# Moving the triangular substitution to GpSimd, a state update by multiply-add, and scan copies planned first

## The chip, the cores and the metric

The kernel runs on one core of one Trainium2 chip. The metric is the device time of one execution in microseconds (us), lower is better. Five engines work side by side, each through its own queue in a fixed order: TensorE (PE, matmuls; PEld is its weight load), VectorE (DVE), ScalarE (ACT), GpSimd (POOL) and SyncE (SP, which here issues the DMAs).

## The reference, cut to what matters

One layer of a hybrid encoder trunk over 1024 tokens of width 1024. A modulated RMSNorm feeds one wide projection; three token mixers read it: an mLSTM, a gated long convolution by FFT, and a bidirectional RWKV-7 scan. Their outputs are gated, projected, merged and added to the input. The change lies in the RWKV-7 branch. Each of its 16 heads carries a 64x64 state, once forwards and once backwards:

```
def step(state, inp):
    r_t, w_t, k_t, v_t, kk_t, a_t = inp
    sa = jnp.einsum('bhij,bhj->bhi', state, -kk_t)
    state = (state * w_t[:, :, None, :] + sa[..., None] * (kk_t * a_t)[:, :, None, :]
             + v_t[..., None] * k_t[:, :, None, :])
    return state, jnp.einsum('bhij,bhj->bhi', state, r_t)
...
y_fwd = rwkv7_scan(r_h, dec_h[:, :, 0], k_dir[:, :, 0], v_h, kk, a_h[:, :, 0], reverse=False)
y_bwd = rwkv7_scan(r_h, dec_h[:, :, 1], k_dir[:, :, 1], v_h, kk, a_h[:, :, 1], reverse=True)
```

## The kernel before, in words

The 1024 tokens are cut into 16 chunks of 64. Within a chunk the recurrence becomes a few 64x64 matmuls if the inverse of a unit triangular matrix is at hand; across chunks the state is handed on. Heads go in 8 pairs (two heads fill 128 partitions, both directions lie side by side), and each pair's chunks are treated in two groups g of 8.

For a pair, `load` and `prep` (L1445, L1534) build the decayed keys and queries `ar`, `bk` for one group and direction. `tphase` (L1597) makes the inverses of one group: matmuls `pq`, a DVE transposition into `Ab` (L1625), a DMA of a start matrix into `Tb` (L1628), then the substitution loop of 31 steps (L1630 to L1638). Step l multiplies a column of `Ab` by a finished row of `Tb` into the scratch tile `tm` and adds `tm` onto the rows below. So there are 62 instructions, each waiting for the one before it, with n*m elements per partition (n = 31-l, m = l//2+1): 2856 for all products and as many for all sums. Two more transpositions (L1641, L1644), the matmuls `pw` and `px`, and ACT copies (the last at L1663) then fill `tt`, which the scan multiplies with.

`scan` (L1740) walks the 16 chunks of a pair. A chunk is a chain: matmuls U; DVE copy `us` (L1769); matmuls SA; copies into `SV` by DVE (L1775) and ACT (L1776); matmuls SN; the new state S1 = (SN + S0) * pc as two DVE instructions (`sn`, L1787 and L1788, by the helper at L476); copies of S1 into `SV` by DVE (L1800) and ACT (L1801), with which the next chunk's U begins. `setup` (L1666) prepares the matrices G and B for two chunks at a time. `outputs` adds up the chunk's result `y`.

Four things set the order. `weave` (L72) traces the scan and, between its steps (four to a chunk), pieces of the other generators: the loop of the own pair's second group is traced from step 8 on, that of the next pair's first group from step 41 on, and matmuls of the big projection (`gemm`, L343, with weights split by ACT at L333 and POOL at L334) are filled in evenly. From the traced program a planner writes each engine's queue: among the instructions that are ready by its own cost estimates it takes the one with the lowest number, which is the place in the traced program; `high_priority(n)` lowers the number by n, `tphase` runs 400 ahead (`TP`), and `in_turn` (L391) keeps a group of matmuls together with 10**6. On the chip each queue then runs strictly in that order. Third, tiles have a fixed number of buffers: `ar` and `bk` have 8, so the next pair's group can only be prepared when the current pair's chunks of that group are done, and the PSUM tile of `banks` (L401) has one buffer, which `pq`, `pw`/`px` and the `pgr` and `ptv` of `setup` take in turn. Fourth, SP's queue issues the DMAs, among them the one into `Tb`.

POOL has little in its queue in the scan: `wl` (L334), the memset of `s` in `prep` (L1555), and in some pairs a few casts.

Of the kernel before, what the change touches and what calls it, by code (L numbers as in the profile page):

```python
# [11 lines left out]
F32 = mybir.dt.float32  # L12
# [13 lines left out]
SA, SB = 100, 16  # L26
# [86 lines left out]
class Row0:  # L113
# [133 lines left out]
    def first(self, w1t, bf):  # L247

        acc = self.ts(w1t[:, 0:1], 0.0, MUL)
        for i in range(1, 17):  # L250
            acc = self.tt(acc, w1t[:, i:i + 1], ADD)
        return self.act(acc, bf, 0)
# [33 lines left out]
class Trunk:  # L286
# [104 lines left out]
    def in_turn(self, calls, ins=None):  # L391

        for f in calls:
            if ins is None:
                ins = f()  # L395
                continue
            with self.tc.issue_after(ins.ins), self.tc.high_priority(10 ** 6):
                ins = f()  # L398
        return ins

    def banks(self, name):  # L401

# [1194 lines left out]
    def tphase(self, cx, g):  # L1597

        nc, rp = self.nc, self.rp
        x2 = lambda n: self.ep.tile([128, 16, 32], F32, name=n, tag="x2", bufs=3)
        q, q21 = x2("quad"), self.ep.tile([128, 16, 32], F32, name="q21", tag="q21", bufs=1)
        pq = [x.rearrange("p (c t) -> p c t", t=CL) for x in self.banks("pq")]

        def blocks():

            for d in range(2):
                for c in range(8):
                    bt, al = cx["bk"][g, d, c], cx["ar"][g, d, c]  # L1610
                    for h in range(2):
                        hs = slice(64 * h, 64 * h + 64)
                        yield partial(nc.tensor.matmul, pq[d][64 * h:64 * h + 32, c, :], bt[hs, 0, 0:32], al[hs, 0, :],
                                      start=True, stop=True)
                        yield partial(nc.tensor.matmul, pq[d][64 * h + 32:64 * h + 64, c, 0:32], bt[hs, 0, 32:64],
                                      al[hs, 0, 32:64], start=True, stop=True)
        self.in_turn(blocks())
        for d, ps in enumerate(pq):
            u = slice(d * 8, d * 8 + 8)
            nc.scalar.copy(q[:, u, :], ps[:, :, 0:32])  # L1620
            for h in range(2):
                nc.scalar.copy(q21[64 * h:64 * h + 32, u, :], ps[64 * h:64 * h + 32, :, 32:64])
        yield
        Ab = self.ep.tile([128, 32, 32], F32, name="Ab", tag="Ab", bufs=1)
        nc.vector.transpose(Ab.rearrange("p t (g u) -> p t g u", g=2),  # L1625
                            q.rearrange("p u t -> p t u").unsqueeze(2).broadcast_to([128, 32, 2, 16]))
        Tb = x2("Tb").rearrange("p a b -> p (a b)").rearrange("p (t s) -> p t s", s=16)
        nc.sync.dma_start(Tb, self.A["tinit"])  # L1628
        tm = rp.tile([128, 136], F32, name="tm", tag="tm", bufs=1)
        for l in range(31):  # L1630
            n, m = 31 - l, l // 2 + 1
            x = tm[:, 0:n * m].rearrange("p (a b) -> p a b", b=m)
            self.tt(x, Ab[:, l + 1:32, l].unsqueeze(2).broadcast_to([128, n, m]),
                    Tb[:, l, 0:m].unsqueeze(1).broadcast_to([128, n, m]))
            o = Tb[:, l + 1:32, 0:m]
            self.tt(o, o, x, ADD)
            if l % 5 == 4:
                yield  # L1638
        tt = self.tt_t[g]
        t1 = x2("t1").rearrange("p a b -> p (a b)").rearrange("p (v s) -> p v s", s=16)  # L1640
        nc.vector.transpose(t1.rearrange("p v s -> p s v"), Tb.rearrange("p t s -> p s t"))  # L1641
        t1 = t1.rearrange("p (g u) s -> p u s g", g=2)
        t2 = x2("t2")
        nc.vector.transpose(t2.rearrange("p u (s g) -> p u s g", g=2), t1)  # L1644
        yield

        W = x2("W")
        pw, px = (x.rearrange("p (u t) -> p u t", t=32) for x in self.banks("pwx"))
        r = [slice(64 * h, 64 * h + 32) for h in range(2)]
        self.in_turn(partial(nc.tensor.matmul, pw[64 * h + 32:64 * h + 64, u, :], q21[r[h], u, :], t1[r[h], u, :],  # L1650
                             start=True, stop=True) for u in range(16) for h in range(2))
        for h in range(2):
            r1, r2 = slice(64 * h, 64 * h + 32), slice(64 * h + 32, 64 * h + 64)
            nc.scalar.copy(W[r2], pw[r2])
            nc.scalar.copy(tt[r1, :, 0:32], t2[r1])
            nc.scalar.copy(tt[r2, :, 32:64], t2[r2])
        yield
        r = [slice(64 * h + 32, 64 * h + 64) for h in range(2)]
        self.in_turn(partial(nc.tensor.matmul, px[64 * h:64 * h + 32, u, :], W[r[h], u, :], t2[r[h], u, :],
                             start=True, stop=True) for u in range(16) for h in (1, 0))  # L1660
        for h in range(2):
            r1 = slice(64 * h, 64 * h + 32)
            nc.scalar.copy(tt[r1, :, 32:64], px[r1])  # L1663
        yield
# [75 lines left out]
    def scan(self, cx, nx):  # L1740

        nc, rp = self.nc, self.rp
        S0 = None
        y = rp.tile([128, T], F32, name="y", tag="y", bufs=1)
        hsl = (slice(0, 64), slice(64, 128))

        def chunk(m):

            G, B, SV, at = cx["set"]
            at = at[m % 2]  # L1750
            step = at[1] - at[0]
            return G, B, SV, at, slice(at[0], at[1] + (1 if step > 0 else -1) if at[1] + step >= 0 else None, step)
        now, late = chunk(0), None
        for m in range(16):
            g, c, j = m // 8, m % 8, m % 2
            tt = self.tt_t[g]
            ar = [cx["ar"][g, d, c] for d in range(2)]
            G, B, SV, at, both = now
            if j == 0:
                ahead = self.setup(cx, m // 2 + 1) if m < 14 else self.setup(nx, 0) if nx else iter(())  # L1760
            ch = self.ps.tile([128, 4, 2, CL], F32, name="pch", tag="c", bufs=2)
            U, SA, SN, py = (ch[:, i] for i in range(4))

            ins = self.in_turn(partial(nc.tensor.matmul, U[hsl[h], d], G[:, j, d, h, 0:64], SV[:, h, at[d]],
                                       start=True, stop=True) for d in range(2) for h in (1, 0))
            if late:
                late[0](ins)
            us = self.sm.tile([128, 2, CL], F32, name="us", tag="us", bufs=2)
            nc.vector.tensor_copy(us, U)  # L1769
            ins = self.in_turn(partial(nc.tensor.matmul, SA[hsl[h], d], tt[hsl[h], 8 * d + c, :], us[hsl[h], d],  # L1770
                                       start=True, stop=True) for d in range(2) for h in range(2))
            if late:
                late[1](ins)
            late = None
            nc.vector.tensor_copy(SV[0:64, 0, both], SA[0:64])  # L1775
            nc.scalar.copy(SV[0:64, 1, both], SA[64:128])  # L1776
            yield
            next(ahead, None)
            yield
            self.in_turn(partial(nc.tensor.matmul, SN[hsl[h], d], B[:, j, d, hsl[h]], SV[:, h, at[d]],  # L1780
                                 start=True, stop=True) for d in range(2) for h in (1, 0))
            S1 = self.sm.tile([128, 2, 64], F32, name="sn", tag="sn", bufs=3)
            pc = cx["pc"][g][:, :, c:c + 1].broadcast_to([128, 2, 64])
            if m == 0:
                self.tt(S1, SN, pc)
            else:
                self.tt(S1, SN, S0, ADD)  # L1787
                self.tt(S1, S1, pc)  # L1788
            late = self.outputs(y, py, m, S0, ar, now)
            S0 = S1  # L1790
            if m < 15:
                now = chunk(m + 1)

            if m in (7, 15):
                late[1](late[0](None))
                late = None
            if m < 15:

                SV, at = now[2], now[4]
                nc.vector.tensor_copy(SV[0:64, 0, at], S1[0:64])  # L1800
                nc.scalar.copy(SV[0:64, 1, at], S1[64:128])  # L1801
            yield
            next(ahead, None)
            yield
        cx["y"] = y
        if nx:
            cx["y"] = self.dram.tile([128, T], F32, name="yd", tag="yd", bufs=2)
            nc.sync.dma_start(cx["y"], y)
# [107 lines left out]
```

## Time and profile before

| what | value |
|---|---|
| three runs, median (lowest to highest) | 2187.35 us (2179.21 to 2191.44) |
| the profiled execution | 2200.05 us |
| its span | 2198.3 us |
| TensorE clock granted, mean | 0.956 |
| scan of the 8 pairs | about 929 to 1990 us of the span |

The profile is one execution. Its times count from the start of the span; 1.75 us of the execution lie outside it. A group of instructions is shown as line, engine, operation, out<-in, shape and count, then busy time and the mean of one in ns, then the idle time of its engine before them and what ended that. A row of one tile has the shortest, the median and the longest duration in ns, and the first and the last start. A row of the timeline has the start and the duration in us, and in brackets the engine's idle time before it.

### The profile page before, as it was taken

The page shows a single profiled execution, that of the slowest core. Times are in us where ns is not written, and L with a number is a line of the kernel's source. Part 1 is how long each engine was busy: PE and PEld are TensorE (multiplying, and loading weights), DVE is VectorE, ACT ScalarE, POOL GpSimd, SP SyncE. Part 2 cuts the span into 40 slices and gives each one's busy share as a digit, 9 for nine tenths or more (in the row PEclk, how much of TensorE's full clock was granted, in tenths as well). Part 3 has the DMA queues.
Part 4 walks back from the last instruction along what each step waited for, and adds up shares of the span by engine and source line. Part 5 has one row for each costly group of instructions (what it writes and reads, how often), then busy time and mean ns, then how long its engine had stood idle before and what let it go on. Part 6 is the DMA issues. An engine that isn't in the chain of part 4 may idle for free. (4 is left out here: it accounts for less than half of the span.)

```text
span 2198.3 us, 45984 instructions
## 1 busy us (share of the span) xinstructions
PE 1994.0 (91%) x17098; PEld 1509.2 (69%) x17098; DVE 1634.6 (74%) x4754; ACT 1103.2 (50%) x2558; POOL 424.3 (19%) x485
## 2 busy tenths in 40 slices
PE   6999899999989899899989999999898887897998
PEld 4666777787868677666766676666666665675786
DVE  4854999988447947788787888868887888764536
ACT  5557356454242115664665756667466564532221
POOL 2211311122222432311101111111114411010200
PEclk9999999999999999999998999999899998897999
DMA  8211222334465345321322333224143542445623
GB/s 255 70 67 59 78 77 90 112 101 127 143 200 172 119 138 163 124 68 61 130 79 93 117 106 102 92 81 136 52 155 118 187 144 63 159 143 175 196 89 129
DMA packets 169384, 262.19 MB, mean 119 GB/s; under 512 B 17863, under 2 KB 87335, under 8 KB 169160
## 3 DMA queue, kind: packets, MB, share of 16 engines
q1 hardware_dynamic: 169160, 259.25, 36.3%
q8 instruction: 135, 2.21, 0.4%
q14 instruction: 89, 0.73, 0.1%
HBM read 181.06 MB, written 78.12 MB: 118 GB/s over the span
## 5 line engine op out<-in xcount | busy, mean ns | idle before, releaser
L334 POOL TENSOR_TENSOR wl<-wraw,wh 128x256 fp32r<-128x256 f32 x408 | 371.5, 915 | 1488.6 <-ACT wh L333 1464.8
L351 PE MATMUL pg<-hh,wh 128*128 128x512 f32 x1440 | 601.5, 418 | 20.9 <-ACT wh L333 11.8
L352 PE MATMUL pg<-hh,wl 128*128 128x512 f32 x1440 | 594.3, 413 | 16.4 <-POOL wl L334 16.3
L353 PE MATMUL pg<-hl,wh 128*128 128x512 f32 x1440 | 592.4, 412 | 1.9 <-DVE hl L565 1.8
L351 PEld LDWEIGHTS pg<-hh,wh 128*128 128x128 f32 x1440 | 278.7, 194 | 88.9 <-ACT wh L333 15.1
L352 PEld LDWEIGHTS pg<-hh,wl 128*128 128x128 f32 x1440 | 279.3, 194 | 78.0 <-POOL wl L334 22.2
L353 PEld LDWEIGHTS pg<-hl,wh 128*128 128x128 f32 x1440 | 278.1, 193 | 62.0 <-DVE hl L565 2.8
L333 ACT CAST wh<-wraw 128x256 fp32r<-128x256 f32 x408 | 162.7, 404 | 220.6 <-PE pg L353 122.1
L476 DVE TENSOR_TENSOR tm<-Ab,Tb 128x126 f32<-128x126 f32 (+22 forms) x496 | 145.4, 293 | 4.4 <-DMA Tb<-in_tinit 2.7
L476 DVE TENSOR_TENSOR Tb<-Tb,tm 128x126 f32<-128x126 f32 (+22 forms) x496 | 144.2, 291 | 1.9
L473 DVE SCALAR_TENSOR_TENSOR st<-pg,hmu,st 128x511 f32<-128x511 f32 (+1 forms) x130 | 80.9, 636 | 27.9 <-ACT e L424 17.6
L476 DVE TENSOR_TENSOR G<-pgr,gmask 128x512 f32<-128x512 f32 x128 | 85.4, 679 | 17.0 <-PE pgr L398 17.0
L457 ACT ACTIVATE st<-pg 128x512 f32<-128x512 f32 x74 | 44.2, 597 | 99.9 <-PE pg L353 95.0
L1684 ACT COPY G<-ar 64x128 f32<-64x128 f32 x256 | 64.3, 295 | 48.4 <-DVE G L476 46.6
L473 DVE SCALAR_TENSOR_TENSOR st<-st,pg 128x512 f32<-128x512 f32 x80 | 54.3, 679 | 35.7 <-PE pg L353 12.7
L398 PE MATMUL pgr<-ar,bk 64*128 64x128 f32 x896 | 76.9, 287 | 0.0
L141 DVE SCALAR_TENSOR_TENSOR row<-row 64x1 f32<-64x1 f32 x393 | 72.7, 208 | 2.1
L1769 DVE COPY us<-pch 128x128 f32<-128x128 f32 x128 | 36.3, 283 | 45.8 <-PE pch L398 45.5
L395 PEld LDWEIGHTS pch<-SV,G 128*64 128x64 f32 x256 | 25.3, 139 | 65.5 <-ACT SV L1801 52.3
L395 PE MATMUL pch<-SV,G 128*64 128x64 f32 x256 | 43.2, 252 | 27.7 <-ACT SV L1801 26.2
L476 DVE TENSOR_TENSOR dw<-dw,dw 128x512 f32<-128x512 f32 x92 | 67.1, 760 | 0.9
L395 PEld LDWEIGHTS pch<-SV,B 128*64 128x64 f32 x256 | 25.3, 139 | 60.1 <-ACT SV L1776 50.1
(677 smaller groups left out, 4228.4 us busy)
## 6 DMA issues: line engine op xcount, KB each, us to landing
wraw<-in_w_in SPq DMA_DIRECT2D x340, 128.0 KB, 2.3
low<-lora SPq DMA_DIRECT2D x32, 512.0 KB, 4.1
sig<-st SPq DMA_DIRECT2D x48, 256.0 KB, 2.6
st<-sig SPq DMA_DIRECT2D x48, 256.0 KB, 3.5
wraw<-in_w_br SPq DMA_DIRECT2D x68, 128.0 KB, 2.8
adw<-in_ada_w SPq DMA_DIRECT2D x16, 512.0 KB, 7.1
x<-in_x SPq DMA_DIRECT2D x8, 512.0 KB, 6.1
hx<-st SPq DMA_DIRECT2D x16, 256.0 KB, 2.0
```

What stands on the lines that cost most here:

```text
L141: self.ops.append(lambda: self.nc.vector.scalar_tensor_tensor(o, a, s, b, op0=op0, op1=op1))
L333: self.nc.scalar.copy(hi, raw)
L334: self.nc.gpsimd.tensor_tensor(lo, raw, hi.bitcast(F32), op=SUB)
L351: nc.tensor.matmul(p, wh, hh, start=(k == 0), stop=False)
L352: nc.tensor.matmul(p, wl, hh, start=False, stop=False)
L353: nc.tensor.matmul(p, wh, hl, start=False, stop=(k == n - 1))
L395: ins = f()
L398: ins = f()
L457: self.nc.scalar.activation(o, p, AF.Tanh, scale=0.5)
L473: return self.nc.vector.scalar_tensor_tensor(out, in0, s, in1, op0=op0, op1=op1)
L476: return self.nc.vector.tensor_tensor(out, a, b, op=op)
L1684: nc.scalar.copy(G[0:64, :, d, h, 0:64], cx["al"][g, d, b % 4][hsl[h]])
```

## The change

Three edits, all in the RWKV-7 branch. The two instructions of each step of the substitution loop are issued on GpSimd and not on VectorE, with the same operands. The new state is formed as S1 = SN * pc + S0d, by one scalar_tensor_tensor for each direction, where S0d = S0 * pc (with this chunk's pc) has been made on GpSimd from the state before, right after that state was ready; the first chunk still has SN * pc alone. And the scan's copies (`us`, both pairs of `SV` copies) and the instructions that make S1 are traced with a priority of 10**6; the multiplication on GpSimd is not.

```
+    def first(self):
+
+        return self.tc.high_priority(10 ** 6)
...
         for l in range(31):
             n, m = 31 - l, l // 2 + 1
             x = tm[:, 0:n * m].rearrange("p (a b) -> p a b", b=m)
-            self.tt(x, Ab[:, l + 1:32, l].unsqueeze(2).broadcast_to([128, n, m]),
-                    Tb[:, l, 0:m].unsqueeze(1).broadcast_to([128, n, m]))
+            nc.gpsimd.tensor_tensor(x, Ab[:, l + 1:32, l].unsqueeze(2).broadcast_to([128, n, m]),
+                                    Tb[:, l, 0:m].unsqueeze(1).broadcast_to([128, n, m]), op=MUL)
             o = Tb[:, l + 1:32, 0:m]
-            self.tt(o, o, x, ADD)
+            nc.gpsimd.tensor_tensor(o, o, x, op=ADD)
...
-            nc.vector.tensor_copy(us, U)
+            with self.first():
+                nc.vector.tensor_copy(us, U)
...
-            nc.vector.tensor_copy(SV[0:64, 0, both], SA[0:64])
-            nc.scalar.copy(SV[0:64, 1, both], SA[64:128])
+            with self.first():
+                nc.vector.tensor_copy(SV[0:64, 0, both], SA[0:64])
+                nc.scalar.copy(SV[0:64, 1, both], SA[64:128])
...
-            pc = cx["pc"][g][:, :, c:c + 1].broadcast_to([128, 2, 64])
-            if m == 0:
-                self.tt(S1, SN, pc)
-            else:
-                self.tt(S1, SN, S0, ADD)
-                self.tt(S1, S1, pc)
+            pc = cx["pc"][g][:, :, c:c + 1]
+            with self.first():
+                if m == 0:
+                    self.tt(S1, SN, pc.broadcast_to([128, 2, 64]))
+                else:
+                    for d in range(2):
+                        self.stt(S1[:, d], SN[:, d], pc[:, d], S0d[:, d])
+            if m < 15:
+
+                S0d = rp.tile([128, 2, 64], F32, name="sd", tag="sd", bufs=2)
+                pc = cx["pc"][(m + 1) // 8][:, :, (m + 1) % 8:(m + 1) % 8 + 1]
+                nc.gpsimd.tensor_tensor(S0d, S1, pc.broadcast_to([128, 2, 64]), op=MUL)
...
-                nc.vector.tensor_copy(SV[0:64, 0, at], S1[0:64])
-                nc.scalar.copy(SV[0:64, 1, at], S1[64:128])
+                with self.first():
+                    nc.vector.tensor_copy(SV[0:64, 0, at], S1[0:64])
+                    nc.scalar.copy(SV[0:64, 1, at], S1[64:128])
```

## Prediction, made blind

> **What bounds the kernel now.** I read the page's first part, then the view by windows, then the timeline of two halves of a pair, and last the rows of the tiles that the change touches. The page:
>
> ```profile
> PE 1994.0 (91%) x17098; PEld 1509.2 (69%) x17098; DVE 1634.6 (74%) x4754; ACT 1103.2 (50%) x2558; POOL 424.3 (19%) x485
> ```
>
> Over the span POOL is the idle engine. Only the scan changes, so the next rows are windows (start and end, length, then busy time and count of PE, PEld, DVE, ACT and POOL, then the granted clock): the stretch just ahead of the scan, the scan, and inside the scan one substitution loop and the 17 us after it.
>
> ```profile
> 866.00:929.00 63.00, 57.07 (x371) 43.61 (x369) 51.47 (x126) 38.58 (x74) 17.81 (x16) 1.00 0.35 119
> 929.00:1990.00 1061.00, 958.49 (x12168) 705.19 (x12167) 845.54 (x2465) 625.80 (x1555) 169.66 (x215) 0.95 0.33 108
> 1262.00:1306.00 44.00, 41.99 (x526) 29.98 (x526) 40.55 (x139) 24.23 (x62) 6.13 (x9) 1.00 0.23 74
> 1306.00:1323.00 17.00, 16.79 (x249) 12.39 (x249) 8.12 (x20) 11.54 (x24) 0.73 (x1) 1.00 0.44 155
> ```
>
> In the scan DVE is busy 80% of the time and PE 90%. But DVE is full only while a loop runs (40.55 of 44 us); behind it DVE is half idle (8.12 of 17) and PE does projection matmuls while the scan stands still. So something other than the load of DVE paces the scan. The timeline of DVE, then of ACT, over two halves of a pair shows it: `us` marks the first chunk of a half, `Ab` and the first and last `tm` and `Tb` the loop, the `tt` copies its end.
>
> ```profile
> 1261.51 0.27 DVE L1769 COPY us<-pch 128x128 f32<-128x128 f32 x1
> ...
> 1269.03 2.00 DVE L1625 STREAM_TRANSPOSE Ab<-quad 128x1024 f32<-128x1024 f32 x1
> ...
> 1271.18 0.19 DVE L476 TENSOR_TENSOR tm<-Ab,Tb 128x31 f32<-128x31 f32 x1
> 1271.30 0.27 DVE L1775 COPY SV<-pch 64x128 f32<-64x128 f32 x1
> 1271.50 0.19 DVE L476 TENSOR_TENSOR Tb<-Tb,tm 128x31 f32<-128x31 f32 x1
> 1271.61 1.22 DVE L1564 TENSOR_TENSOR_SCAN s<-smask,s 128x520 f32<-128x520 f32 x1
> ...
> 1305.69 0.16 DVE L476 TENSOR_TENSOR Tb<-Tb,tm 128x16 f32<-128x16 f32 x1
> ...
> 1322.68 0.69 DVE L1498 TENSOR_SCALAR a<-phs 128x512 f32<-128x512 f32 x1 [1.06 <-PE phs L1433]
> 1323.29 0.28 DVE L1769 COPY us<-pch 128x128 f32<-128x128 f32 x1
> ...
> 1335.43 1.99 DVE L1625 STREAM_TRANSPOSE Ab<-quad 128x1024 f32<-128x1024 f32 x1
> ...
> 1337.45 0.21 DVE L476 TENSOR_TENSOR tm<-Ab,Tb 128x31 f32<-128x31 f32 x1
> 1337.69 0.21 DVE L476 TENSOR_TENSOR Tb<-Tb,tm 128x31 f32<-128x31 f32 x1
> ...
> 1378.28 0.16 DVE L476 TENSOR_TENSOR Tb<-Tb,tm 128x16 f32<-128x16 f32 x1
> ...
> 1394.50 0.29 DVE L1769 COPY us<-pch 128x128 f32<-128x128 f32 x1 [1.08 <-PE pch L398]
> ```
>
> ```profile
> 1314.45 1.17 ACT L1663 COPY tt<-pwx 32x512 f32<-32x512 f32 x2
> ...
> 1386.78 1.15 ACT L1663 COPY tt<-pwx 32x512 f32<-32x512 f32 x2
> ```
>
> ```profile
> L1625 DVE STREAM_TRANSPOSE Ab<-quad x16: 1952/1986/2106, 866.9 to 1895.7; 128x1024 f32<-128x1024 f32 x16
> ```
>
> Each half is one ring of five stretches. From its first `us` to `Ab`: 7.5 and 12.1 us, mean 9.8. `Ab` to the first `tm`: 2.1. The loop: 34.7 and 41.0, mean 37.8. From there to the end of the `tt` copies: 9.8 and 9.5, mean 9.6. From there to the next half's `us`: 7.7 and 6.6, mean 7.1. Sum 66.5 us; the 16 `Ab` lie (1895.7 - 866.9) / 15 = 68.6 us apart, so these two halves stand for all. The ring closes through buffers: the next group's `bk` waits for the chunks of the group before, and G and `pgr` of the next chunks wait for the PSUM tile that `pw` and `px` hold. The loop is over half of it. On DVE it is slow because other DVE work stands between its links (1271.18, 1271.30, 1271.50, 1271.61), not because its instructions are.
>
> **Part one: the loop on POOL.**
>
> ```profile
> 929.00:1990.00 1061.00, 271.06 (x930) 0.95 0.33 108
> ```
>
> This is the window view for the tile `tm`: 930 instructions, 15 loops of 62, take 271 us of DVE. All leave DVE's queue. What they cost on POOL no row shows; the nearest are POOL's own (tile rows with shortest, median and longest ns; a group; a memset; one line of the timeline):
>
> ```profile
> L334 POOL TENSOR_TENSOR wl<-wraw,wh x408: 715/742/10347, 34.0 to 2091.0; 128x256 fp32r<-128x256 f32 x136
> L930 POOL TENSOR_TENSOR dml<-kt,dmh x4: 1272/1286/1297, 636.4 to 640.6; 128x512 fp32r<-128x512 f32 x4
> L334 POOL TENSOR_TENSOR wl<-wraw,wh 128x256 fp32r<-128x256 f32 x165 | 140.4, 854 | 773.2 <-ACT wh L333 753.2 <-PE ptv L1693 11.3 <-issue 4.5
> L1555 POOL MEMSET s<- x32: 106/113/120, 747.0 to 1829.9; 128x8 f32 x32
> 1664.52 1.18 POOL L334 TENSOR_TENSOR wl<-wraw,wh 128x256 fp32r<-128x256 f32 x1 [0.22 <-POOL wl L334]
> ```
>
> 256 more elements cost 1286 - 742 = 544 ns, 2.125 ns each, which leaves 198 ns for the instruction. A loop is 62 x 0.198 + 5712 x 0.002125 = 12.3 + 12.1 = 24.4 us (from below, with the memset's 113 ns as the constant, 19.1). To this comes the hand-over from each to the next: 0.03 us on DVE (1337.45 + 0.21 to 1337.69), at most the 0.22 of the one POOL row. I take 0.08, nearer to DVE, since the POOL row may hold a second wait: 5.0 us. In the scan `wl` takes 854 ns on average against 742, 112 ns for waiting on DVE; DVE loses most of its two-input work, so I take half, 0.056 x 62 = 3.5. Strangers in POOL's queue: 165 `wl` in 1061 us are 5.9 in 38 us, 4.4 us; the new S0d has 128 elements, 0.47 us, about 4.6 of them, 2.2. These fill ten of the hand-overs, -0.8. Loop: 38.7 us, 0.9 more than now. Far ends: 19.1 + 1.9 + 0 + 4.4 = 25 and 24.4 + 13.6 + 6.9 + 6.6 = 51.
>
> Queues: the loop is put behind and ahead of `wl`, the memsets of `s` and `SV`, and S0d. While its first instruction waits for `Ab` or for the DMA into `Tb`, `wl` waits behind it, and so PE's matmuls with `wl`; the idle time in the row (773 of 1061 us) is the cover. No DMA moves; SP's queue keeps its order.
>
> The Trainium skill, "SBUF — State Buffer", section "Who interferes with whom", says that a DVE instruction with two SBUF inputs and a GpSimd one that reads SBUF exclude each other for a whole instruction. The trace agrees (`wl` has 10347 ns at the longest), and by the rule the loop comes out as in the second slower rival below.
>
> **Part two: the new state.** Rows of the tiles `sn`, `SV`, `y`, and one scalar_tensor_tensor from PSUM:
>
> ```profile
> L476 DVE TENSOR_TENSOR sn<-pch,sn x120: 236/287/294, 941.3 to 1985.8; 128x128 f32<-128x128 f32 x120
> L476 DVE TENSOR_TENSOR sn<-sn,pc x120: 236/284/858, 943.4 to 1986.2; 128x128 f32<-128x128 f32 x120
> L1800 DVE COPY SV<-sn x120: 171/209/1305, 935.5 to 1982.2; 64x128 f32<-64x128 f32 x120
> L476 DVE TENSOR_TENSOR y<-y,pch x128: 165/210/226, 1002.6 to 1987.7; 128x64 f32<-128x64 f32 x128
> L473 DVE SCALAR_TENSOR_TENSOR E<-pnm,cols,cmask x64: 322/334/352, 276.1 to 408.9; 128x128 f32<-128x128 f32 x64
> ```
>
> Two dependent instructions, 0.57 us, become two independent ones of 64 columns, between 0.21 (`y`) and 0.33 (`E`) each; I take 0.24, 0.48 in all: -0.1 us a chunk. S0d is ready long before, unless POOL lags: it has the time of U, SA and SN. If it is late, DVE's queue stops at the first multiply-add with `prep` behind it, and the copies of S1 wait.
>
> **Part three: copies first.** Only the planned order changes. A scan instruction on DVE can now be passed by none that is ready: the `us` at 1323.29 stood behind an `a<-phs` of 0.69 us. I take 0.3 us saved for each of five scan instructions of a chunk, with 0 and 0.69 as ends. Inside the ring's loop the scan isn't on the path; outside, about two chunks of each half are: 2 x (5 x 0.3 + 0.1) = 3.2 us. `prep` and G, passed by now, are the price; DVE, lighter by 271 us, pays it.
>
> **Sum.** A half changes by 0.9 - 3.2 = -2.3 us, 15 halves by -35. The first loop lies ahead of the scan (DVE 51.47 of 63 us busy) and the last eight chunks have no loop behind them: I count both at nothing, since what the one may lose (0.9) the other gains (8 x 0.1). Of the profiled execution's 2200.05 us (span 2198.3, and 1.75 around it) 2165 are left; the median of the runs is 0.9942 of it, so 2152.
>
> **The rivals.** Slower by the hand-over (0.15): POOL's wait for itself is 0.22 us. That adds 62 x 0.14 = 8.7 to each loop, a half is 6.4 longer, 15 x 6.4 = +96: 2296, 2283 as a median. It decides from 0.08 + 2.3 / 62 = 0.12 us on. For it speaks the one row; against it that DVE needs 0.03.
>
> Slower by the shared port (0.13): if each POOL instruction of the loop meets half of a two-input DVE instruction, like this one,
>
> ```profile
> L476 DVE TENSOR_TENSOR bk<-tmp,s x64: 394/412/952, 854.8 to 1864.9; 128x256 f32<-128x256 f32 x64
> ```
>
> it costs 0.21 x 62 = 13.0 in place of 3.5; a half is 7.2 longer, +108: 2308, as a median 2295. It decides where half of them are hit. For it: `SV<-sn`, 209 ns, once took 1305. Against it: most `wl` take their 742.
>
> No change (0.17): the copies were seldom late or the path runs through ACT and `setup` at the restart, so the 3.2 us aren't there, and the loop is as long as now. Then 2187, and it is also the case that the priority does nothing.
>
> Much faster (0.15): the constant is the memset's, hand-over 0.03: 19.1 + 1.9 + 3.5 + 4.4 + 2.2 - 0.3 = 30.8, 7.0 less; a half -10.2, in all -153. PE's 958 of 1061 us busy, though by modelled ends, leave 103: about -100, 2100, as a median 2088.
>
> **How the numbers follow.** My forecast has 0.40, with its own range of 2120 to 2176. Measurement tells 0.5% (11 us) from no change. Faster: 0.40 + 0.15 = 0.55; same 0.17; slower 0.28. The range leaves out a tenth on each side, the fastest of the last rival with the lowest loop and the slow ones above their prices: 2080 to 2285.
>
> **What would show it.** The tiles `tm` and `Tb` on POOL, mean near 0.39 us; loop near 39 us from first `tm` to last `Tb`; `Ab` 66 us apart and not 68.6; DVE's busy time in the scan near 845 - 271 - 0.1 x 120 = 560; no wait of the scan for S0d over half a microsecond. Wrong: `Ab` over 69 us apart, or gaps over 0.12 us between POOL's links, or scan instructions on DVE stretched beside POOL, as `SV<-sn` was.

## The result, and the profile after

The changed kernel takes 2418.28 us (median of 4 runs, 2415.08 to 2425.05) where the kernel before, on the same chip, takes 2187.38. The ratio is 1.1065 with a 95% interval of 1.1025 to 1.1105: slower by 231 us, where 2152 was forecast. The profiled execution has a span of 2413.3 us against 2198.3. First the page, then three windows: the scan, one loop, and the part of that loop in which VectorE stands (columns as in the prediction).

```profile
PE 2014.5 (83%) x17098; PEld 1517.7 (63%) x17098; DVE 1441.0 (60%) x3762; ACT 1100.2 (46%) x2556; POOL 846.5 (35%) x1597
```

```profile
960.00:2200.00 1240.00, 960.10 (x11755) 698.20 (x11753) 643.20 (x1495) 608.89 (x1503) 546.22 (x1193) 0.88 0.28 90
1330.00:1364.00 34.00, 16.03 (x147) 11.85 (x145) 11.25 (x28) 8.55 (x21) 28.51 (x69) 0.73 0.13 40
1348.00:1363.60 15.60, 2.30 (x21) 1.89 (x17) 0.39 (x2) 0.03 (x1) 13.43 (x37) 0.50 0.06 20
```

The same work (PE 2014.5 us busy, 1994.0 before) is spread over a longer time. Before, DVE was busy for 40.55 of the 44 us of a loop and PE for 41.99. Now for half of a loop nothing runs but POOL: DVE has 0.39 us of work in 15.60, PE 2.30, and PE's granted clock there is 0.50. The rows of the loop itself show nothing slow (groups, then one tile's row):

```profile
L1640 POOL TENSOR_TENSOR Tb<-Tb,tm 128x126 f32<-128x126 f32 (+22 forms) x496 | 204.0, 411 | 35.6
L1637 POOL TENSOR_TENSOR tm<-Ab,Tb 128x126 f32<-128x126 f32 (+22 forms) x496 | 196.0, 395 | 49.9 <-DVE Ab L1629 8.9
```

```profile
L1629 DVE STREAM_TRANSPOSE Ab<-quad x16: 1899/2026/2101, 854.2 to 2083.7; 128x1024 f32<-128x1024 f32 x16
```

The links take 395 and 411 ns, as predicted (0.39 us). But `Ab` comes every (2083.7 - 854.2) / 15 = 82.0 us, not 68.6. What lies in between is in the list of waits (engine, tile and line that waits, what it waits for: us in total, times, longest):

```profile
DVE t L1645 <- POOL Tb L1640: 229.6, 16, 20.2
ACT tt L1659 <- DVE t L1648: 193.4, 14, 17.4
...
DVE sn L477 <- POOL sd L1800: 60.9, 12, 8.4
...
PEld pg L352 <- POOL wl L334: 26.6, 16, 9.5
```

The transposition behind the loop (L1641 before) waits for the loop's end, all 16 times, for 229.6 us. No such wait stood in the list of before. There the loop's last `Tb` (1305.69 us, shown with the prediction) was followed on VectorE by this, without an idle gap before the transposition:

```profile
1306.32 0.29 DVE L1769 COPY us<-pch 128x128 f32<-128x128 f32 x1 [0.47 <-PE pch L398]
1306.53 1.10 DVE L1641 STREAM_TRANSPOSE t<-Tb 128x512 f32<-128x512 f32 x1
```

The timelines of DVE and of POOL over one loop of the changed kernel show the stop:

```profile
1328.62 2.03 DVE L1629 STREAM_TRANSPOSE Ab<-quad 128x1024 f32<-128x1024 f32 x1 [1.52 <-ACT quad L1624]
...
1346.17 0.47 DVE L477 SCALAR_TENSOR_TENSOR sn<-pch,pc,sd 128x64 f32<-128x64 f32 x2 [5.82 <-POOL sd L1800]
...
1347.63 0.69 DVE L477 SCALAR_TENSOR_TENSOR st<-st,pg 128x512 f32<-128x512 f32 x1 [0.51 <-ACT st L461]
1363.53 1.05 DVE L1645 STREAM_TRANSPOSE t<-Tb 128x512 f32<-128x512 f32 x1 [15.21 <-POOL Tb L1640]
1364.48 0.25 DVE L1774 COPY us<-pch 128x128 f32<-128x128 f32 x1
```

```profile
1330.73 0.26 POOL L1637 TENSOR_TENSOR tm<-Ab,Tb 128x31 f32<-128x31 f32 x1 [1.08 <-DVE Ab L1629]
1331.06 0.27 POOL L1640 TENSOR_TENSOR Tb<-Tb,tm 128x31 f32<-128x31 f32 x1
...
1345.74 0.40 POOL L1800 TENSOR_TENSOR sd<-sn,pc 128x128 f32<-128x128 f32 x1
...
1363.28 0.22 POOL L1640 TENSOR_TENSOR Tb<-Tb,tm 128x16 f32<-128x16 f32 x1
```

From 1348.3 on DVE's next instruction is the transposition, and it needs the last `Tb`. DVE works its queue in order, so the next chunk's `us`, which needs nothing of the loop, stands behind it until 1364.48: 16 us in which the scan has nothing to do, and PE almost nothing. Before, the loop stood in the same queue as the transposition, so whatever the planner put between `Ab` and `t` ran beside the links. Counted in the timelines, 5.3 `us` copies lie between `Ab` and `t` before, as a mean over 15 loops, and 2.1 after. The rest of the half's chunks now comes behind the loop, on the path.

### The profile page after: what moved, and what is told of

Same layout as the page of the kernel before. It is cut to its first block, busy times and chain, and to the rows that moved or that the text cites. A ratio compares the mean times of both kernels' runs of the same rounds, so it can differ in the third digit from the quotient of the medians.

```text
span 2413.3 us, 46180 instructions
## 1 busy us (share of the span) xinstructions
PE 2014.5 (83%) x17098; PEld 1517.7 (63%) x17098; DVE 1441.0 (60%) x3762; ACT 1100.2 (46%) x2556; POOL 846.5 (35%) x1597
## 4 chain that ended last, share of the span: by engine, by line
PE 44%; POOL 21%; DVE 12%; issue 9%; ACT 7%; DMA 7%; SPq 1%; POOLq 0%; DVEq 0%; ACTq 0%
POOL Tb L1640 9%; PE pg L351 8%; POOL tm L1637 8%; PE pg L352 8%; PE pg L353 8%; PE pout L1263 3%; PE pch L398 3%; POOL wl L334 3%; PE pch L395 2%; DMA wraw<-in_w_in 1%; PE pG L957 1%; DVE st L477 1%; PE pwx L398 1%; DVE dw L480 1%; DVE s L1568 1%
## 5 line engine op out<-in xcount | busy, mean ns | idle before, releaser
L334 POOL TENSOR_TENSOR wl<-wraw,wh 128x256 fp32r<-128x256 f32 x408 | 347.9, 857 | 916.0 <-ACT wh L333 904.0
L351 PE MATMUL pg<-hh,wh 128*128 128x512 f32 x1440 | 615.7, 428 | 20.1 <-ACT wh L333 12.8
L1640 POOL TENSOR_TENSOR Tb<-Tb,tm 128x126 f32<-128x126 f32 (+22 forms) x496 | 204.0, 411 | 35.6
L1637 POOL TENSOR_TENSOR tm<-Ab,Tb 128x126 f32<-128x126 f32 (+22 forms) x496 | 196.0, 395 | 49.9 <-DVE Ab L1629 8.9
L1800 POOL TENSOR_TENSOR sd<-sn,pc 128x128 f32<-128x128 f32 x120 | 55.6, 463 | 338.1 <-DVE sn L477 284.4
L1645 DVE STREAM_TRANSPOSE t<-Tb 128x512 f32<-128x512 f32 x16 | 16.9, 1055 | 229.6 <-POOL Tb L1640 229.6
L477 DVE SCALAR_TENSOR_TENSOR sn<-pch,pc,sd 128x64 f32<-128x64 f32 x240 | 56.6, 276 | 134.3 <-POOL sd L1800 60.9
L395 PE MATMUL pch<-us,tt 64*64 64x64 f32 x256 | 44.1, 255 | 91.5 <-DVE us L1774 91.3
L1659 ACT COPY tt<-t 32x512 f32<-32x512 f32 x32 | 19.7, 615 | 193.6 <-DVE t L1648 193.4
L395 PEld LDWEIGHTS pch<-us,tt 64*64 64x64 f32 x256 | 25.7, 140 | 120.5 <-DVE us L1774 101.2
```

The lines of the kernel that those rows point to most:

```text
L334: self.nc.gpsimd.tensor_tensor(lo, raw, hi.bitcast(F32), op=SUB)
L351: nc.tensor.matmul(p, wh, hh, start=(k == 0), stop=False)
L477: return self.nc.vector.scalar_tensor_tensor(out, in0, s, in1, op0=op0, op1=op1)
L1637: nc.gpsimd.tensor_tensor(x, Ab[:, l + 1:32, l].unsqueeze(2).broadcast_to([128, n, m]), Tb[:, l, 0:m].unsqueeze(1).broadcast_to([128, n, m ...
L1640: nc.gpsimd.tensor_tensor(o, o, x, op=ADD)
```

## The experiments

Theory A: the loss is this stop of VectorE's queue at an instruction that waits for GpSimd. Rival B: the decayed state S0d, late in GpSimd's queue behind the loop's links (1345.74 above), holds the scan. Rival C: a loop on GpSimd costs its time wherever VectorE's instructions stand, at first by the shared memory port, which would stretch the instructions of both engines. Ratios are to runs of the kernel before on the same chip (medians 2184.7 to 2189.7 us).

### One part alone

**e1_loop_only**: the kernel before with the two `tensor_tensor` of the loop on `nc.gpsimd`, nothing else.

> Only the substitution loop is put on GpSimd; the state update and the priorities are those of the kernel before. Theory A (VectorE's queue stands still at the transposition behind the loop, 229.6 us in the trace of after): most of the loss stays, 2340 to 2400 us, and VectorE again waits over 180 us for the loop at that transposition. Rival B (the state decayed ahead waits in GpSimd's queue behind the loop and holds up the scan): that instruction is gone, so 2150 to 2210 us. Rival C (the shared port: GpSimd and VectorE stretch each other's instructions): 2340 to 2400 us too, but with VectorE's two-input instructions over 20% longer than before.

2417.41 us, ratio 1.104 (1.0973 to 1.1106): the whole loss, without S0d and without priorities, and 17 us above the range of A.

```profile
DVE t L1641 <- POOL Tb L1636: 269.6, 15, 20.2
```

The sign of rival C is missing: VectorE's instructions with two inputs in SBUF are not 20% longer. As means, `sn<-sn,pc` goes from 311 to 355 ns, `bk<-a,s` from 456 to 495, `bk<-tmp,s` from 430 to 436, and `ar<-r,P` falls from 465 to 438.

**e4_decay_on_act**: the changed kernel with S0d taken off GpSimd.

```
-                nc.gpsimd.tensor_tensor(S0d, S1, pc.broadcast_to([128, 2, 64]), op=MUL)
+                for d in range(2):
+                    nc.scalar.activation(S0d[:, d], S1[:, d], AF.Copy, scale=pc[:, d])
```

> The whole change, but the decayed state is made on ScalarE by two activations with a per-partition scale, so that it never stands behind the loop. Theory A: only the 60.9 us of waits for that state can go, and what VectorE gains it gives back at the transposition: 2350 to 2420 us. Rival B: 2150 to 2210 us. Rival C: 2340 to 2420 us.

2433.8 us, ratio 1.1114 (1.1045 to 1.1184), 14 us above the range of A and far from that of B.

```profile
DVE t L1645 <- POOL Tb L1640: 257.0, 15, 21.1
```

Without the wait for S0d the wait at the transposition is longer by about half of it (257.0 against 229.6). Rival B falls as the cause of the change's loss.

**e2_no_loop**: the changed kernel with the loop back on VectorE (`self.tt`), new state and priorities kept.

> Everything of the change but the loop, which stays on VectorE. Theory A: no loss is left, and the saving of the prediction's second and third part shows by itself, 2150 to 2190 us. Rival B: where GpSimd has no loop the decayed state is in time, so also 2150 to 2200 us. Rival C: no GpSimd load, 2150 to 2200 us. If the priorities themselves did harm, over 2220 us.

2246.59 us, ratio 1.0263 (1.0214 to 1.0312). Theories A, B and C expected no loss; it is the last case named, harm by the priorities, that came. Two runs split it. **e6_first_only** keeps the priorities alone, **e11_state_only** the new state alone (`first()` returns an empty context), both with the loop on VectorE.

> This is the changed kernel with two of its three parts taken back: the 62 instructions of the inverses' loop stand on VectorE, and the state is the old sum and product on VectorE; only the priority of the scan's copies and state is left. With the loop on VectorE the run before last was 2246.6 us against 2189.7, its loop 41.7 us against 38.0 and the way from the half's first copy to the transposition in front of the loop 12.8 us against 10.3. Theory P (the priority does it: what is passed by belongs to the next half's inverses, which are on the path): 2230 to 2260 us, loop above 41 us. Theory S (the new state does it: its product on GpSimd is waited for): 2170 to 2200 us here, and the loss in the run with the new state alone.

2233.45 us, ratio 1.0199 (1.0155 to 1.0244).

> The complement: only the new state is left (the decayed state on GpSimd, two multiply-adds on VectorE); the loop stands on VectorE and nothing has priority. Theory P: 2165 to 2200 us. Theory S: 2230 to 2260 us, with VectorE's multiply-adds waiting for the decayed state, or GpSimd's other work held up behind that product (286 us of wait in 67 places in the run with priority and new state).

2196.63 us, ratio 1.0041 (1.0014 to 1.0067). So theory P holds: the priorities cost 2.0% by themselves, the state 0.4%. How the priorities lose is in DVE's timeline of e6_first_only:

```profile
1291.85 0.29 DVE L1774 COPY us<-pch 128x128 f32<-128x128 f32 x1
...
1297.97 0.29 DVE L1774 COPY us<-pch 128x128 f32<-128x128 f32 x1
...
1304.43 0.29 DVE L1774 COPY us<-pch 128x128 f32<-128x128 f32 x1
...
1310.11 0.27 DVE L1774 COPY us<-pch 128x128 f32<-128x128 f32 x1
...
1314.64 0.29 DVE L1774 COPY us<-pch 128x128 f32<-128x128 f32 x1 [0.24 <-PE pch L398]
...
1321.30 0.75 DVE L480 TENSOR_TENSOR Tb<-Tb,tm 128x16 f32<-128x16 f32 x1
...
1337.40 0.29 DVE L1774 COPY us<-pch 128x128 f32<-128x128 f32 x1 [0.27 <-PE pch L398]
```

The chunks do hurry (4.5 to 6.5 us apart here), and then stand for 22.8 us, from 1314.64 to 1337.40, for the next group's inverse. As means over the halves, the chunks of a half start 6.3 us apart and the next half 25.7 us after its last chunk; before, 7.7 and 13.0. Over 15 halves the loop takes 40.4 us against 38.0, and the way from a half's first `us` to `Ab` 13.0 against 10.3. What the scan gains on VectorE, the ring loses.

### The transposition queued later

**e3_late_transposition**: the changed kernel, with both transpositions traced in the half's eighth chunk and ordered behind that chunk's DVE copy into `SV`. In the kernels below only the place differs.

```
+        yield
         tt = self.tt_t[g]
+        with self.tc.issue_after(self.mark.ins) if self.mark else ExitStack():
...
-            nc.vector.tensor_copy(SV[0:64, 0, both], SA[0:64])
+            self.mark = nc.vector.tensor_copy(SV[0:64, 0, both], SA[0:64])
...
-                put(ahead(tc, self.tphase(cx[i], 1), TP), *range(6, 28, 2))
+                put(ahead(tc, self.tphase(cx[i], 1), TP), *range(6, 22, 2), 28, 29, 30, 31)
```

> The whole change, but the transpositions behind the loop are traced four chunks later and queued on VectorE behind the scan's copies of the last chunk of the half, so that five to six chunks stand between Ab and them, as before, and not two. Theory A: the loss is gone, 2120 to 2200 us, and the wait at the transposition falls from 229.6 us to under 60. Rival B: the decayed state is still late, 2330 to 2420 us. Rival C: the loop is as long and the port as loaded, 2330 to 2420 us.

2348.08 us, ratio 1.0724 (1.0662 to 1.0786). The expectation of A (2120 to 2200 us) failed, and the time lies in the range that B and C had named. The wait at the transposition is gone, but only 70 of the 231 us come back: it now starts 17.9 us after the loop's end, and another wait has grown from 60.9 us:

```profile
DVE sn L478 <- POOL sd L1803: 146.5, 30, 9.4
...
PEld pg L353 <- POOL wl L335: 62.3, 26, 12.7
```

To be rid of S0d and the priorities, the next two move the loop alone and put the transpositions behind the seventh chunk's copy (**e9_loop_only_t6**) or the sixth's (**e10_loop_only_t5**).

> The kernel before with the loop on GpSimd, nothing else of the change, and the two transpositions behind the loop queued on VectorE behind the copy of the half's seventh chunk instead of where the planner put them (some two chunks behind the transposition in front of the loop). Theory A (the loss of the change comes from the place of this transposition in VectorE's in-order queue): the wait of 270 us in 15 goes under 60 us in all, and the time to 2150 to 2260 us, from 2417. Rival C (a loop on GpSimd costs this kernel its time wherever VectorE's instructions stand, by the shared memory port or by holding back GpSimd's other work): above 2350 us.

2326.79 us, ratio 1.063 (1.0594 to 1.0666).

> The same with the two transpositions behind the copy of the sixth chunk, one chunk earlier. Theory A: a chunk beside the loop takes some 8 us, the loop 31 us, and the transposition in front of it comes about one to two chunks into the half, so the loop ends about at the sixth chunk: waits under 100 us in all, and 2130 to 2230 us, below the run with the seventh chunk, since the scan's last chunk stands free beside the copies behind the transposition. Rival C: above 2350 us.

2346.49 us, ratio 1.0716 (1.0677 to 1.0755). Both lie between the theories: above A's range, below or at the edge of C's. In e9 the wait for the loop has shrunk to two places, and a different one stands in the list; the timeline of POOL, then of PE, shows one of its places:

```profile
DVE t L1644 <- POOL Tb L1637: 21.5, 2, 18.5
...
PEld pg L353 <- POOL wl L335: 153.7, 37, 15.0
```

```profile
1346.03 2.11 POOL L335 TENSOR_TENSOR wl<-wraw,wh 128x256 fp32r<-128x256 f32 x3
```

```profile
1346.81 0.80 PE L353 MATMUL pg<-hh,wl 128*128 128x512 f32 x1 [3.86 <-POOL wl L335]
```

Three `wl` come in one go as soon as the loop has left POOL (the transposition that needs its end starts at 1346.11), and PE, which also runs in order, stood for the first of them with the scan's matmuls behind. This is a second queue that stops, and in the changed kernel it was hidden behind the first: `wl` was waited for 26.6 us there, 24.9 before.

### GpSimd left to the loop

The g kernels put the rest of GpSimd's work in the scan on VectorE as well.

```
-        self.nc.gpsimd.tensor_tensor(lo, raw, hi.bitcast(F32), op=SUB)
+        self.nc.vector.tensor_tensor(lo, raw, hi.bitcast(F32), op=SUB)
...
-        nc.gpsimd.memset(s[:, :, 0:1], 0.0)
+        nc.vector.memset(s[:, :, 0:1], 0.0)
...
-                nc.gpsimd.memset(SV[0:64], 0.0)
+                nc.vector.memset(SV[0:64], 0.0)
```

**g1_clear_seventh**: this and e9.

> The kernel before with the loop on GpSimd, the transpositions behind it queued on VectorE behind the copy of the half's seventh chunk, and the other work of GpSimd in this stage (the low parts wl of the weights, the zeroing of s and of SV) moved to VectorE, so that nothing waits in GpSimd's queue behind a loop. Without that last part it took 2326.8 us, with 153.7 us in 37 places in which TensorE stood for a wl (24.9 us in 18 in the kernel before). Theory A2 (two in-order queues stop: VectorE at the transposition and GpSimd's queue at the loop, and each wait shows only when the other is gone): the wait for wl goes under 40 us, the half to 62 to 70 us from 76.9, the time to 2100 to 2220 us. Rival C (the loop on GpSimd takes its toll in another way, the shared port or ScalarE's copies): above 2290 us.

2199.75 us, ratio 1.008 (1.0054 to 1.0106): 127 us less than e9 and within the range of theory A with two queues; rival C falls. The edit moves `wl` and both memsets together; in e9 the list of waits has 2.1 us for a memset of GpSimd and 153.7 for `wl`.

```profile
DVE t L1644 <- POOL Tb L1637: 40.4, 9, 17.4
...
PEld pg L353 <- DVE wl L335: 31.8, 20, 7.7
```

**g3_clear_planned**: the same with the transpositions where the planner puts them.

> The same with the transpositions where the planner puts them. Theory A2: the wait of VectorE for the loop stays (270 us in 15 with the loop alone moved), so 2370 to 2430 us; GpSimd's other work by itself is not the cause of the change's loss. If the late low parts were the first cause, this would fall below 2300 us.

2436.76 us, ratio 1.116 (1.1098 to 1.1223). That is 7 us above its range: clearing GpSimd's queue alone gives nothing back; the wait at the transposition is all there.

```profile
DVE t L1641 <- POOL Tb L1636: 292.3, 16, 20.0
```

**i2_before_clear** asks what that clearing costs by itself: the kernel before with those three lines alone.

> The kernel before with the low parts wl and the zeroings of s and SV on VectorE, the loop there too. 408 low parts at some 0.5 to 0.7 us are 200 to 290 us more for VectorE over the whole kernel, some 10 us in a half of 68 us in which VectorE is the engine of the inverses' loop: 2250 to 2330 us if VectorE's time in the scan's stage is the bound, about 2190 if it has that much slack.

2190.25 us, ratio 1.0018 (0.9997 to 1.0039): nothing that can be told, so g1 may be read as the price of the loop.

Then the place. **g2_clear_sixth** is behind the sixth chunk's copy of SA, **h1_between** behind the sixth chunk's last copy of the state, **h2_first_copy** behind the seventh's `us`, **i1_seventh_last** behind the seventh's last copy of the state.

> The same with the transpositions behind the sixth chunk's copy. With VectorE's wait for the loop at 67 us in 8 places in the run with the sixth chunk and GpSimd's other work left there, theory A2 expects 2100 to 2240 us, at most 30 us from the run with the seventh. Rival C: above 2290 us.

2250.08 us, ratio 1.0302 (1.0258 to 1.0347): 10 us above the range, and 50 us above g1, more than the 30 expected.

> The run with the loop on GpSimd, its other work moved away and the transpositions behind the loop queued behind the sixth chunk's last copy of the state (between the two places that gave 2199.8 and 2250.1 us). If the place is all that is left, the transposition starts 1 to 3 us after the loop's end instead of 5.4, VectorE stands some 2 us a loop, and the half is 64 to 67 us instead of 67.3: 2150 to 2195 us. If the place no longer decides, 2195 to 2250 us.

2233.06 us, ratio 1.0222 (1.0184 to 1.0261).

> The same, behind the seventh chunk's first copy (us), some 2 us ahead of the place that gave 2199.8 us. If the place is all that is left: 2165 to 2200 us, the second transposition then standing behind the seventh chunk's copy of SV. If not: 2195 to 2230 us.

2213.78 us, ratio 1.0124 (1.0083 to 1.0164).

> The loop on GpSimd, its other work on VectorE, the transpositions behind the seventh chunk's last copy of the state, some 4 us later than in the run of 2199.8 us (loop's end 46.8 us into the half, transposition 52.2 there). If the ring of the inverses is what now decides, 4 us a half come on top: 2220 to 2260 us. If VectorE's stop at the transposition was still the larger price, another 10 us are gained: 2180 to 2195 us.

2187.42 us, ratio 1.0009 (0.999 to 1.0027). I had looked for the best place between the sixth and the seventh chunk (h1 and h2 came out as their second case, i1 as VectorE's stop being the larger price); it lies later. In the order of the queue the times are 2250, 2233, 2214, 2200 and 2187 us, and VectorE's mean idle time at the transposition 4.1, 2.9, 2.5, 1.5 and 0.6 us a loop. So the stop of VectorE costs more than the inverse gains by a transposition that starts sooner (52.2 us into the half in g1, 55.2 in i1, by the sums of the table below). At the last place the loop on GpSimd is as fast as the kernel before, and no version measured is faster.

```profile
L1626 DVE STREAM_TRANSPOSE Ab<-quad x16: 1936/1988/2106, 872.3 to 1863.4; 128x1024 f32<-128x1024 f32 x16
```

```profile
DVE t L1644 <- POOL Tb L1637: 26.3, 7, 16.9
```

### The whole change, treated in the same way

**g4_change_clear_seventh** is the changed kernel with g1's edits; **g5_no_priority** is g4 without the priorities, **g7_decay_on_act** is g4 with S0d on ScalarE.

> The whole change (loop on GpSimd, new state with its decayed product on GpSimd, priorities) with the transpositions behind the seventh chunk's copy and the low parts and zeroings on VectorE; only the loop and the decayed state are left on GpSimd. The decayed state stands in GpSimd's queue among the loop's instructions, and VectorE waited 146.5 us in 30 places for it where the transposition had been put late. Theory A2: those waits stay, 2200 to 2320 us, slower by 40 us or more than the run without the state and the priorities. Rival D (the state and the priorities are harmless or useful as soon as nothing else stops): within 20 us of that run or below it.

2316.43 us, ratio 1.0609 (1.0571 to 1.0647): 117 us above g1, so rival D falls.

```profile
DVE sn L478 <- POOL sd L1803: 156.7, 30, 7.4
...
DVE t L1648 <- POOL Tb L1641: 17.5, 1, 17.5
```

> The whole change with late transpositions and GpSimd's other work moved (2316.4 us), without the priorities. If the priorities cause the remaining loss: 2200 to 2240 us. If the decayed state behind the loop's instructions does: 2270 to 2320 us, with the 156.7 us of wait of VectorE for it still there.

2312.48 us, ratio 1.0579 (1.0535 to 1.0623), with 158.3 us of wait for S0d.

> The same as the run of 2316.4 us, priorities kept, with the decayed state formed by two instructions of ScalarE, so that GpSimd has the loop alone. If the priorities cause the remaining loss: 2270 to 2320 us. If the decayed state in GpSimd's queue does: 2200 to 2250 us.

2264.56 us, ratio 1.0354 (1.0301 to 1.0407), between its two expectations. So here S0d in GpSimd's queue costs 2316 - 2265 = 52 us, and the priorities nothing that shows. Rival B names a real cost after all, a third one in the same form: an in-order queue (VectorE's, at the multiply-add) behind a GpSimd that is busy with links. It shows once the larger stop is gone. The other 65 us of g7 over g1 belong to the priorities, the new state or its two ScalarE instructions together; that was not split further. VectorE's wait at the transposition may be part of it: 57.1 us in 13 places in g7, 40.4 in 9 in g1.

The stretches of the ring, as means over 15 halves, read off the timelines' rows of `us`, `Ab`, `tm`, `Tb`, `t` and `tt` (us):

| kernel | `us` to `Ab` | to `tm` | loop | to `t` | to end of `tt` | to next `us` | half | DVE idle at `t` |
|---|---|---|---|---|---|---|---|---|
| before | 10.3 | 2.4 | 38.0 | 0.4 | 8.5 | 8.4 | 68.0 | 0.0 |
| after | 14.5 | 3.0 | 31.8 | 0.0 | 17.9 | 15.6 | 82.9 | 14.0 |
| e6_first_only | 13.0 | 2.3 | 40.4 | 0.3 | 8.6 | 6.2 | 70.8 | 0.0 |
| e3_late_transposition | 15.3 | 2.9 | 33.1 | 17.9 | 9.2 | -0.1 | 78.3 | 0.0 |
| e9_loop_only_t6 | 12.1 | 2.8 | 32.7 | 14.4 | 9.8 | 5.2 | 76.9 | 0.2 |
| g1_clear_seventh | 11.1 | 2.3 | 33.4 | 5.4 | 9.4 | 5.7 | 67.3 | 1.5 |
| i1_seventh_last | 12.4 | 2.2 | 33.6 | 7.0 | 9.9 | 1.6 | 66.7 | 0.6 |

## Why the prediction was wrong

**The step that failed** is in "The loop on POOL". The prediction read the ring as five stretches of which one changes: "Loop: 38.7 us, 0.9 more than now", and the stretches behind it, 9.6 and 7.1 us, stayed as they were. It wrote "All leave DVE's queue" and asked only what stands behind the loop in POOL's queue. It did not ask which instruction on VectorE now waits for another engine, where that instruction stands, and what is queued behind it. That is the first transposition behind the loop (L1641, in the changed kernel L1645), there two chunks behind `Ab`, with the scan behind it. The loop shrank by 6.2 us a half. But the stretch from its end to the end of `tt` grew from 8.9 to 17.9 and the one from there to the next `us` from 8.4 to 15.6, since the chunks that used to run beside the loop now run after it; the first stretch, to `Ab`, grew by 4.2 as well (by 2.7 with the priorities alone in e6, by 1.6 with the loop alone in e1). The half is 14.9 us longer, 15 halves 224 us.

That the planner put the transposition there because it holds GpSimd's instructions for shorter than they are is argued, not shown: its estimates leave no record in a trace. Shown is the place (2.1 chunks, not 5.3) and what moving it does.

**The price of the links** was right: 24.4 us predicted for the 62 of them, (196.0 + 204.0) / 16 = 25.0 measured, with the port's share in it; a hand-over of 0.08 assumed, 0.078 measured as the median from the end of a `tm` to the start of its `Tb`. So the rival by hand-over, +96 us, falls.

**The port** was taken at 3.5 us a loop; the changed kernel paid 2.0. In its trace a link with no VectorE instruction beside it takes nearly the same time whenever its shape comes (428 to 447 ns for the `Tb` of 126 elements), and the others can be held against the median of these. 105 links had a VectorE instruction with two SBUF inputs beside them and took 303 ns more, as a mean; 200 had only others beside them and took 12 ns more. That is 105 x 0.303 / 16 = 2.0 us a loop. In i1_seventh_last, where VectorE works on and has `wl` as well, it is 420 links with 213 ns, 5.6 us a loop, against 321 with 6 ns, and all links take 461 ns as a mean and not 403:

```profile
L1637 POOL TENSOR_TENSOR Tb<-Tb,tm 128x126 f32<-128x126 f32 (+22 forms) x496 | 238.5, 481 | 38.8
L1634 POOL TENSOR_TENSOR tm<-Ab,Tb 128x126 f32<-128x126 f32 (+22 forms) x496 | 218.6, 441 | 687.8 <-DMA wraw<-in_w_in 217.0 <-DVE Ab L1626 200.6 <-ACT a L1496 56.9
```

One such link, and the VectorE instruction that starts with it:

```profile
1298.12 0.31 POOL L1634 TENSOR_TENSOR tm<-Ab,Tb 128x70 f32<-128x70 f32 x1
1298.51 0.61 POOL L1637 TENSOR_TENSOR Tb<-Tb,tm 128x70 f32<-128x70 f32 x1
```

```profile
1298.51 0.43 DVE L335 TENSOR_TENSOR wl<-wraw,wh 128x256 fp32r<-128x256 f32 x1 [1.43 <-ACT wh L334]
```

The rule of the Trainium skill ("SBUF — State Buffer", section "Who interferes with whom") that VectorE with two SBUF inputs and a GpSimd instruction that reads SBUF exclude each other agrees with this. The rival that charged half of a 412 ns instruction to every link, +108 us, falls: a hit costs what it said or more, but 105 of 960 links were hit (420 of 960 in i1). The `wl` of 10347 ns that the prediction showed is the same thing at its worst: it began at 757.60 us among eighteen `dw` of VectorE with two SBUF inputs, one behind the other from 756.45 to 767.36, and ended at 767.95.

**Visitors.** I took 6.6 us of `wl` and S0d in a loop, less 0.8. The changed kernel's loop of 31.8 us leaves 31.8 - 25.0 - 62 x 0.08 = 1.8: less of them came than I took (38 `wl` and 32 S0d started inside 15 loops, where I had 5.9 and 4.6 a loop). The cost that I did not see is that of what stands behind the loop. "The idle time in the row (773 of 1061 us) is the cover" is true as long as VectorE's stop hides it, and false without: 153.7 us of PE's time in e9. A queue that is idle on average is still shut for 32 us at a stretch.

**S0d** "is ready long before, unless POOL lags". It lagged: 60.9 us of wait in 12 places, against the sign "no wait of the scan for S0d over half a microsecond". The mechanism named there, VectorE's queue stopping at the first multiply-add, is what g4 shows, at 52 us.

**Copies first** was to save 3.2 us a half. With the loop on VectorE it costs (2233.45 - 2188.14) / 15 = 3.0 us a half. The reason given, that a lighter VectorE pays for what is passed by, would fit: with the loop gone from VectorE the priorities made no difference (2316.43 and 2312.48). It is not shown, since in that pair the wait for S0d may hide one.

**The ends of the kernel** I counted at nothing. The rows of `us`, before and after:

```profile
L1769 DVE COPY us<-pch x128: 236/285/294, 929.5 to 1983.3; 128x128 f32<-128x128 f32 x128
```

```profile
L1774 DVE COPY us<-pch x128: 236/291/293, 908.1 to 2194.6; 128x128 f32<-128x128 f32 x128
```

The scan begins 21.4 us sooner. Its span grows from 1053.8 to 1286.5, by 232.7, and what follows the last `us` by 3.7: 232.7 + 3.7 - 21.4 = 215.0, the whole difference of the spans (2413.3 - 2198.3).

**The expected gain** does not come even where every stop but 0.6 us a loop is taken away. In i1 the half is 66.7 us, eight chunks of 8.3, and in the kernel before 68.0; the 4.4 us that the loop is shorter are given back between its end and `t` (7.0 against 0.4). PE's busy share is the same 91% of the span in both. What holds the half near 67 us then, PE or the chain of the chunks, was not settled.

## What to carry to other kernels

A chain that moves to another engine turns its first reader on the old engine into a wait across engines. Find that reader's place in its queue, list what is queued behind it, and compare the chain's length with the independent work in front of it; do the same for every other job of the engine that receives the chain. When one such stop goes, look for the next: here three lay behind one another (`t`, `wl`, S0d), and the later two were small in the list of waits (26.6 and 60.9 us) until the first was gone (153.7 in e9, 156.7 in g4).

## What the runs showed of the hardware beside this

What a short `tensor_tensor` of GpSimd costs can be read by shape. The changed kernel's rows have

```profile
L1640 POOL TENSOR_TENSOR Tb<-Tb,tm 128x126 f32<-128x126 f32 x48 | 21.6, 450 | 3.1
...
L1640 POOL TENSOR_TENSOR Tb<-Tb,tm 128x16 f32<-128x16 f32 x16 | 3.5, 220 | 1.2
```

The mean of 450 holds links that VectorE held up; the 34 of the 48 with no VectorE instruction beside them have a median of 432. That is 220 ns for 16 elements a partition and (432 - 220) / 110 = 1.9 ns for each one more; the wait for its own last result adds 0.078 us. And the clock that PE was granted was lower where PE stood: 0.50 in the 15.6 us in which it was busy for 2.30, 0.922 as a mean of the changed kernel (83% busy), 0.959 in i1_seventh_last (91%).
